# Queueing the side work of ScalarE and VectorE behind the weight chunk where it is traced, in a decoder-trunk kernel at S = 256

## The chip, the core and the metric

The kernel runs on one core of a Trainium2 chip. Its time is the device time of one execution in microseconds (us); where several runs are given, the median is used. Profiles come from a single profiled execution of the kernel.

## What is computed

One decoder layer on a 256 x 2048 float32 input (weights float32 too), then a final RMSNorm:

```python
u = rms_norm(x, attn_norm)
proj = u @ w_in                  # split: fox q|k|v|f, MLA latents, GDN q|k|v, z, b, a, three gates
o_fox = fox_mixer(...)           # 8 heads, causal softmax with cumulative forget-gate bias
o_mla = mla_mixer(...)           # 8 heads, latents projected up, rotary part, causal softmax
o_gdn = gdn_mixer(...)           # short conv, SiLU, gated delta rule in chunks of 64, norm * silu(z)
gates = sigmoid(gate)            # three gates of D_MODEL columns
merged = gates[0]*(o_fox @ w_branch[0]) + gates[1]*(o_mla @ w_branch[1]) + gates[2]*(o_gdn @ w_branch[2])
x = x + merged @ w_out
h = rms_norm(x, mlp_norm)
x = x + square(relu(h @ w_up)) @ w_down      # d_ff = 8192
return rms_norm(x, final_norm)
```

## The kernel before

The work is a stream of weight chunks. A chunk is two row tiles of 128 by up to 512 columns of a weight matrix (512 KB). For each, `gemm` (its body runs from L228 to L258) issues one load `raw` on the SP queue (L240, four buffers), rounds it on ScalarE to `wh` (L243, three buffers) and takes the rest `wl = raw - wh` on VectorE (L244, three buffers). TensorE then runs 12 matmuls for it: two row tiles of the weight, two 128-row tiles of the activation, and the three products `uH*wh` (L249), `uH*wl` (L250) and `uL*wh` (L251), which give back the float32 product. There are 590 chunks, numbered c0 to c589 here: the latents and the small columns of w_in (c0 to c23), the fox columns (c24 to c85, with the MLA projections between them), the z columns (c86 to c109, 344 to 360 columns wide), the GDN columns (c110 to c157), the gate columns (c158 to c253), the three branches by four column blocks (c254 to c301), w_out (c302 to c333), and four times w_up and w_down (from c334).

All other work is side work. It is written as generators, and `weave` takes one step of a generator after each chunk of the main stream:

```python
def weave(main, side):
    for _ in main:
        next(side, None)
```

Two more paths lead into the stream. The evacuation of a finished block (`evac`) is traced in `gemm` right after its last chunk. And `later(steps, f)` puts a callback off by so many chunks; `tick` calls it. The order in which a program is written (traced) is not the order in which an engine runs it: a scheduler with a model of the engines' times places each instruction of an engine's list, so a step may stand some chunks earlier on its engine than where it was traced. Each engine then runs its own list strictly in order, so an instruction that waits for a transfer holds up all that stand behind it on that engine, weight casts included.

The places that matter below:

- `turned` (L1043 to L1049) turns a 256 x 512 block so that its columns lie on partitions: VectorE transposes 32 x 32 blocks, POOL's queue writes them to DRAM (`turn`, L1045) and reads them back in four pieces (`zy`, L1048), and `later(TURN, ...)` with TURN = 9 hands the result on, to `halves_of` (L1057 on ScalarE casts the high half, for `mH`, `hH` and `dH`) or, behind w_out, to `gained` (L1100 on ScalarE multiplies by the norm's gain) and then `halves_of`.
- The delta-rule generator `gdn`: `E` holds decays that come back from DRAM by a broadcast load and are used by VectorE at L762. A loop of L838 and L840 on VectorE solves 16 rows step by step; its result goes to DRAM (`td`, L844) and back in eight pieces (`DT`, L854), both on POOL's queue, and VectorE takes it at L863 (`D`), on which 32 x 32 matmuls at L871 wait.
- The gates: `gate_evac` (L986) scales a block by `rstd` (ScalarE L319 for 12 of the 24 evacuations, VectorE L321 for the other 12) and stores it to `gd` (L987, POOL's queue). In the branch stage `evac` loads a gate back (L1066), applies the sigmoid (L1067, ScalarE) and multiplies.
- Fox attention runs as a side generator: bias at L655 (VectorE), scores at L385 and L391 (VectorE), exponent at L388 (ScalarE), transposes at L399 (evacuated by ScalarE) and output at L406 (ScalarE).
- `reload` brings the fox and the MLA output back from DRAM (`of`, `om`, 1 MB each, L1017), and L1084 loads x again for the residual (`xx`, two of 1 MB, POOL's queue).

Of the kernel before, what the change touches and what calls it, by code (L numbers as in the profile page):

```python
# [3 lines left out]

# [53 lines left out]
def decoder_kernel(ctx: ExitStack, tc: tile.TileContext, x, attn_norm, w_in, fox_fgate_bias, mla_q_norm,  # L58
# [30 lines left out]
    def t2(s="t2", dt=F32):  # L89
        return tp.tile([P, 512], dt, tag="t2", name=nm(s), bufs=8)  # L90
# [118 lines left out]
    CK = 2  # L209

    pending = []

    def later(steps, f):

# [2 lines left out]
    def tick():  # L217
        for p in pending:
            p[0] -= 1
        while pending and pending[0][0] <= 0:  # L220
            pending.pop(0)[1]()

    def by_tile(f):

        return lambda k, t: f(k)[:, t * P:(t + 1) * P]

    def gemm(lhsH, lhsL, W, row0, KT, blocks, evac, pair=False):

        ks = {}
        order = [(bi, kc) for bi in range(len(blocks)) for kc in range(0, KT, CK)]  # L230
        if pair:
            order.sort(key=lambda o: (max(o[0], 1), o[0] < 2 and o[1] >= LATE))
        for bi, kc in order:
            c0, n = blocks[bi]
            if kc == 0:
                ks[bi] = [pm.tile([P, 512], F32, tag="mm", name=nm("mm")) for _ in range(2)]
            ps = ks[bi]
            raw = wp.tile([P, CK, 512], F32, tag="raw", name=nm("raw"), bufs=4)
            r0 = row0 + kc * P
            nc.sync.dma_start(out=raw[:, :, :n], in_=W[r0:r0 + CK * P, c0:c0 + n].rearrange("(k p) n -> p k n", p=P))  # L240
            wh = wp.tile([P, CK, 512], F32R, tag="wh", name=nm("wh"), bufs=3)
            wl = wp.tile([P, CK, 512], F32R, tag="wl", name=nm("wl"), bufs=3)
            A.copy(out=wh[:, :, :n], in_=raw[:, :, :n])  # L243
            V.tensor_tensor(out=wl[:, :, :n], in0=raw[:, :, :n], in1=wh[:, :, :n].bitcast(F32), op=ALU.subtract)  # L244
            for kk in range(CK):
                k = kc + kk
                for t in range(2):
                    last = k == KT - 1
                    PE.matmul(ps[t][:, :n], lhsT=lhsH(k, t), rhs=wh[:, kk, :n], start=(k == 0), stop=False)  # L249
                    PE.matmul(ps[t][:, :n], lhsT=lhsH(k, t), rhs=wl[:, kk, :n], start=False, stop=False)  # L250
                    PE.matmul(ps[t][:, :n], lhsT=lhsL(k, t), rhs=wh[:, kk, :n], start=False, stop=last)  # L251
            tick()
            if kc + CK == KT:
                for t in range(2):
                    evac(bi, t, ps[t][:, :n])
            yield
# [28 lines left out]
            for _ in g:  # L285
                pass

    def weave(main, side):

        for _ in main:  # L290
            next(side, None)

    def wait(n):
        return range(n)
# [7 lines left out]
    def w_cols(blocks, evac):  # L302
        return gemm(by_tile(uH), by_tile(uL), w_in, 0, 16, blocks, evac)
# [12 lines left out]
    def scaled_evac(o, i, t):  # L316
        evc[0] += 1
        if evc[0] % 2:
            A.activation(out=o, in_=i, func=AF.Copy, scale=rstd[:, t:t + 1])  # L319
        else:  # L320
            V.tensor_scalar(out=o, in0=i, scalar1=rstd[:, t:t + 1], scalar2=None, op0=ALU.mult)  # L321
# [394 lines left out]
    def gdn():  # L716
# [38 lines left out]
        yield  # L755
        nc.gpsimd.dma_start(out=E, in_=gcd.unsqueeze(0).broadcast_to([P, 16 * P]))
        Ev = E.rearrange("p (u i) -> p u i", u=16)
        for _ in wait(5):
            yield
        for g in range(0, 16, 4):  # L760
            for u in range(g, g + 4):
# [89 lines left out]
        for b in range(4):  # L851
            for f in range(2):
                r0 = 32 * b + 16 * f
                nc.gpsimd.dma_start(out=DT[r0:r0 + 16, :, 32 * b:32 * b + 32], in_=tdv[f, b])  # L854
        for _ in wait(9):
            yield


# [124 lines left out]
    def gates(b0, b1):  # L983
        def gate_evac(bi, t, ps):
            e = me("ge")
            scaled_evac(e, ps, t)  # L986
            nc.gpsimd.dma_start(out=gd[t * P:(t + 1) * P, (b0 + bi) * 512:(b0 + bi + 1) * 512], in_=e)  # L987

        return w_cols([(C_GATE + i * 512, 512) for i in range(b0, b1)], gate_evac)
# [3 lines left out]
    fox_cols = [(i * 512, 512) for i in range(6)]  # L993
    side = chain(x_prep(), load_vectors())
    next(side)
    weave(gemm_first(w_in, blocks[0][0], blocks[0][1], lat_evac), side)
    weave(w_cols(blocks[2:], lambda bi, t, ps: lat_evac(2, t, ps)), side)
    side = chain(mla_prep(), fox_decay())
    weave(w_cols(fox_cols[0:1], fox_evac_at(0)), side)
    run(mla_proj())  # L1000
# [11 lines left out]
    def reload(d, s, r):  # L1012
        H = big(s + "H", F32R).rearrange("p (h t) -> p h t", t=S)
        L = big(s + "L", F32R).rearrange("p (h t) -> p h t", t=S)
        o = big(s)
        r.extend((H, L))
        nc.sync.dma_start(out=o, in_=d)  # L1017
        o = o.rearrange("p (h t) -> p h t", t=S)
        for _ in wait(2):
            yield  # L1020
        for h in range(0, 8, 2):
            hs = slice(h, h + 2)
            A.copy(out=H[:, hs, :], in_=o[:, hs, :])
            V.tensor_tensor(out=L[:, hs, :], in0=o[:, hs, :], in1=H[:, hs, :].bitcast(F32), op=ALU.subtract)
            if h % 4:
                yield
# [34 lines left out]
    for n in range(4):  # L1061
        acc = [t2("acc") for _ in range(2)]
        for i, b in enumerate((2, 0, 1)):
            def evac(bi, t, ps, b=b, n=n, acc=acc, i=i):
                g = t2("gate")
                nc.gpsimd.dma_start(out=g, in_=gd[t * P:(t + 1) * P, b * DM + n * 512:b * DM + (n + 1) * 512])  # L1066
                A.activation(out=g, in_=g, func=AF.Sigmoid)  # L1067
                if i == 0:
                    V.tensor_tensor(out=acc[t], in0=ps, in1=g, op=ALU.mult)
                else:  # L1070
                    V.tensor_tensor(out=g, in0=ps, in1=g, op=ALU.mult)
                    V.tensor_tensor(out=acc[t], in0=acc[t], in1=g, op=ALU.add)
                if i == 2 and t == 1:
                    turned(acc, lambda y: halves_of(y, n, mHt, mLt))

            if n == 0 and b < 2:
                run(again[b])
            weave(gemm(by_tile(lambda k, b=b: o_b[b][0][:, k, :]), by_tile(lambda k, b=b: o_b[b][1][:, k, :]), w_branch[0, b], 0, 8,
                       [(n * 512, 512)], evac), chain(*again))


    x2 = [big(f"xx{t}") for t in range(2)]
    for t in range(2):
        nc.gpsimd.dma_start(out=x2[t], in_=x[t * P:(t + 1) * P, :])  # L1084
    hH, hL, hHt, hLt = hl_pair("h")
    ss2 = small([P, 2, 4], "ss2")

# [12 lines left out]
            A.activation(out=yv[:, k], in_=yv[:, k], func=AF.Copy, scale=gcol[:, 16 + 4 * n + k:17 + 4 * n + k])  # L1100
        halves_of(y, n, hHt, hLt)

    run(gemm(by_tile(mH), by_tile(mL), w_out[0], 0, 16, [(n * 512, 512) for n in range(4)], out_evac, True))
    r2 = rstd_of(ss2, 4, DM, "r2")
    r2s = small([P, 2], "r2s")
    V.tensor_tensor(out=r2s, in0=r2, in1=r2, op=ALU.mult)


    fg = big("fg")
    ss3 = small([P, 2, 4], "ss3")  # L1110
    for c in range(4):
        dH, dL, dHt, dLt = hl_pair("d")
        if c == 2:
            nc.sync.dma_start(out=fg, in_=final_norm.unsqueeze(0).broadcast_to([P, DM]))
        rr = {}

        def up_evac(n, t, ps):
# [3 lines left out]
            if t == 1:  # L1121
                turned([rr[0], rr[1]], lambda y: halves_of(y, n, dHt, dLt))

        run(gemm(by_tile(hH), by_tile(hL), w_up[0], 0, 16, [(c * 2048 + n * 512, 512) for n in range(4)], up_evac, c == 0))

        def down_evac(n, t, ps):
            xb = x2[t][:, n * 512:(n + 1) * 512]
# [69 lines left out]
```

## Time and profile before

| | us |
|---|---|
| median of 3 runs | 1701.19 |
| lowest, highest of them | 1699.45, 1702.70 |
| the profiled execution's own time | 1702.46 |
| its span from first to last instruction | 1700.7 |

| engine | busy, us | share of the span |
|---|---|---|
| PE (TensorE) | 1674.5 | 98% |
| VectorE (DVE) | 1037.1 | 61% |
| ScalarE (ACT) | 803.0 | 47% |
| POOL | 114.2 | 7% |

The mean granted clock of TensorE is 0.995 of full speed. The DMA engines moved 356.53 MB, 210 GB/s on the mean. Matmuls overlap in the records (each is shown with 0.39 us and the next starts some 0.23 us later), so the end of a matmul says less than the start of the next.

### The profile page before, as it was taken

How to read it: one execution, taken by the hardware profiler on the slowest of the kernel's cores; microseconds unless marked ns; L12 is line 12 of the kernel's file. 1: busy time of each engine (PE TensorE's matmuls, PEld its weight loads, DVE VectorE, ACT ScalarE, POOL GpSimd, SP SyncE). 2: the span in 40 equal slices, each digit the busy share in tenths (PEclk: the TensorE clock that was granted, in tenths of full speed). 3: DMA queues.
4: the chain of work that ended last, by engine and by line, in shares of the span. 5: the costliest groups of instructions: out<-in, count | busy, mean ns of one | idle time of the engine just before them, and what ended most of it. 6: DMA issues, size and time to landing. Idle time of an engine off the chain costs nothing.

```text
span 1700.7 us, 21432 instructions
## 1 busy us (share of the span) xinstructions
PE 1674.5 (98%) x7987; PEld 1403.7 (83%) x7987; DVE 1037.1 (61%) x1430; ACT 803.0 (47%) x1035; POOL 114.2 (7%) x204
## 2 busy tenths in 40 slices
PE   9999999999999999999999989999999999999997
PEld 9998889978788788888888778888888888888886
DVE  5755465677679845746666556555655556555655
ACT  5545446556534434544454545433443344434443
POOL 0000000000010100001110101100110011001100
PEclk9999999999999999999999999999999999999999
DMA  7765554766667755877887778756886688667763
GB/s 234 205 172 176 163 171 135 229 193 181 172 177 215 208 162 159 261 217 256 279 294 240 237 200 247 241 192 197 233 262 205 193 234 246 198 191 229 238 208 137
DMA packets 188601, 356.53 MB, mean 210 GB/s; under 512 B 17704, under 2 KB 38608, under 8 KB 187344
## 3 DMA queue, kind: packets, MB, share of 16 engines
q1 hardware_dynamic: 174592, 309.23, 59.9%
q0 software_dynamic: 13584, 45.39, 8.9%
q8 instruction: 62, 1.02, 0.3%
q10 hardware_dynamic: 320, 0.53, 0.1%
q14 instruction: 43, 0.35, 0.1%
HBM read 331.50 MB, written 23.61 MB: 209 GB/s over the span
## 4 chain that ended last, share of the span: by engine, by line
PE 83%; DMA 6%; issue 4%; DVE 4%; ACT 1%; POOL 1%; SPq 0%; DVEq 0%; ACTq 0%; POOLq 0%
PE mm L250 24%; PE mm L251 24%; PE mm L249 24%; DMA zy<-turn 3%; DVE wl L244 2%; ACT wh L243 1%; DVE fs L838 1%; POOL zy L1048 1%; DMA turn<-zy 1%; DMA raw<-in_w_down_dram 1%; DMA of<-of_d 1%; DMA E<-gcd 0%; PE bf L490 0%; PE bf L489 0%; PE bf L488 0%
## 5 line engine op out<-in xcount | busy, mean ns | idle before, releaser
L244 DVE TENSOR_TENSOR wl<-raw,wh 128x1024 fp32r<-128x1024 f32 (+3 forms) x552 | 662.6, 1204 | 501.6 <-ACT wh L243 498.2
L243 ACT CAST wh<-raw 128x1024 fp32r<-128x1024 f32 (+3 forms) x552 | 570.0, 1036 | 671.4 <-PE mm L251 624.6
L250 PE MATMUL mm<-wl,uH 128*128 128x512 f32 (+3 forms) x896 | 346.3, 387 | 2.1 <-DVE wl L244 2.0
L251 PE MATMUL mm<-wh,uL 128*128 128x512 f32 (+3 forms) x896 | 342.8, 383 | 0.0
L249 PE MATMUL mm<-wh,uH 128*128 128x512 f32 (+3 forms) x896 | 318.9, 386 | 1.2 <-ACT wh L243 1.2
L250 PE MATMUL mm<-wl,hH 128*128 128x512 f32 x512 | 200.4, 391 | 2.0 <-DVE wl L244 2.0
L251 PE MATMUL mm<-wh,hL 128*128 128x512 f32 x512 | 199.9, 390 | 0.0
L250 PEld LDWEIGHTS mm<-wl,uH 128*128 128x128 f32 x896 | 168.9, 188 | 32.9 <-DVE wl L244 3.5
L249 PEld LDWEIGHTS mm<-wh,uH 128*128 128x128 f32 x896 | 167.9, 188 | 31.4 <-ACT wh L243 1.7
L251 PEld LDWEIGHTS mm<-wh,uL 128*128 128x128 f32 x896 | 168.8, 188 | 29.6
L250 PE MATMUL mm<-wl,dH 128*128 128x512 f32 x480 | 187.0, 390 | 0.1
L251 PE MATMUL mm<-wh,dL 128*128 128x512 f32 x480 | 186.8, 389 | 0.0
L249 PE MATMUL mm<-wh,hH 128*128 128x512 f32 x512 | 179.2, 391 | 3.5 <-ACT wh L243 3.5
L249 PE MATMUL mm<-wh,dH 128*128 128x512 f32 x480 | 167.2, 389 | 0.0
L249 PEld LDWEIGHTS mm<-wh,hH 128*128 128x128 f32 x512 | 96.3, 189 | 24.4 <-ACT wh L243 4.6
L250 PEld LDWEIGHTS mm<-wl,hH 128*128 128x128 f32 x512 | 96.4, 188 | 23.8 <-DVE wl L244 3.7
L251 PEld LDWEIGHTS mm<-wh,hL 128*128 128x128 f32 x512 | 96.5, 189 | 20.0
L250 PEld LDWEIGHTS mm<-wl,dH 128*128 128x128 f32 x480 | 90.1, 188 | 19.6 <-DVE wl L244 0.9
L251 PEld LDWEIGHTS mm<-wh,dL 128*128 128x128 f32 x480 | 90.1, 188 | 18.7
L249 PEld LDWEIGHTS mm<-wh,dH 128*128 128x128 f32 x480 | 90.1, 188 | 18.6
L1048 POOL DMA_DIRECT2D zy<-turn x96 | 52.4, 553 | 100.1 <-ACT wh L243 37.7
L1045 POOL DMA_DIRECT2D turn<-zy x24 | 13.3, 556 | 657.6 <-DVE zy L1043 657.6
(420 smaller groups left out, 1762.3 us busy)
## 6 DMA issues: line engine op xcount, KB each, us to landing
raw<-in_w_in_dram SPq DMA_DIRECT2D x192, 512.0 KB, 3.9
raw<-in_w_up_dram SPq DMA_DIRECT2D x128, 512.0 KB, 4.4
raw<-in_w_down_dram SPq DMA_DIRECT2D x128, 512.0 KB, 4.5
raw<-in_w_branch_dram SPq DMA_DIRECT2D x48, 512.0 KB, 4.6
raw<-in_w_out_dram SPq DMA_DIRECT2D x32, 512.0 KB, 5.1
turn<-zy POOLq DMA_DIRECT2D x24, 512.0 KB, 3.3
zy<-turn POOLq DMA_DIRECT2D x96, 128.0 KB, 5.8
gd<-ge POOLq DMA_DIRECT2D x24, 256.0 KB, 4.6
```

The source lines that it names most:

```text
L243: A.copy(out=wh[:, :, :n], in_=raw[:, :, :n])
L244: V.tensor_tensor(out=wl[:, :, :n], in0=raw[:, :, :n], in1=wh[:, :, :n].bitcast(F32), op=ALU.subtract)
L249: PE.matmul(ps[t][:, :n], lhsT=lhsH(k, t), rhs=wh[:, kk, :n], start=(k == 0), stop=False)
L250: PE.matmul(ps[t][:, :n], lhsT=lhsH(k, t), rhs=wl[:, kk, :n], start=False, stop=False)
L251: PE.matmul(ps[t][:, :n], lhsT=lhsL(k, t), rhs=wh[:, kk, :n], start=False, stop=last)
L838: V.tensor_tensor(out=tmp[:, :, 0:i + 1], in0=T[:, :, 0:i + 1], in1=Nb[:, 0:i + 1, i].unsqueeze(1).broadcast_to([P, 16, i + 1]), op=ALU.mult)
L1045: nc.gpsimd.dma_start(out=d, in_=z)
L1048: nc.gpsimd.dma_start(out=y[32 * j:32 * j + 32].rearrange("a (g x) -> a g x", g=4), in_=dv[j])
```

## The change

`gemm` remembers the cast and the subtraction of the latest chunk. All side work that is traced afterwards, by `weave` and by `later`, is put behind them: an ordering edge makes the instructions of such a step follow `wh` on ScalarE's list and `wl` on VectorE's. It is a lower bound: the scheduler may still place them further back. The first two weaves (`x_prep`, `load_vectors`) are left free, and evacuations aren't bound. Besides, all 24 gate evacuations become one ScalarE sigmoid with `rstd` as its scale, and the sigmoids of the branch stage go; gate tiles are loaded before their block begins instead of in its evacuation; `of`, `om`, `xx` and the final gain come in pieces of 256 KB, one a step, `xx` on the SP queue instead of POOL's; and two counts of idle steps ahead of `E` and `D` change (5 to 7, 9 to 7).

```diff
+    anchor = []
+    @contextmanager
+    def behind():
+        with ExitStack() as st:
+            for i in anchor:
+                st.enter_context(tc.issue_after(i))
+            yield
...
         while pending and pending[0][0] <= 0:
-            pending.pop(0)[1]()
+            with behind():
+                pending.pop(0)[1]()
...
-            A.copy(out=wh[:, :, :n], in_=raw[:, :, :n])
-            V.tensor_tensor(out=wl[:, :, :n], in0=raw[:, :, :n], in1=wh[:, :, :n].bitcast(F32), op=ALU.subtract)
+            h = A.copy(out=wh[:, :, :n], in_=raw[:, :, :n])
+            l = V.tensor_tensor(out=wl[:, :, :n], in0=raw[:, :, :n], in1=wh[:, :, :n].bitcast(F32), op=ALU.subtract)
+            anchor[:] = [h.ins, l.ins]
...
-    def weave(main, side):
+    def weave(main, side, free=False):
         for _ in main:
-            next(side, None)
+            if free:
+                next(side, None)
+            else:
+                with behind():
+                    next(side, None)
...
-        for _ in wait(5):
+        for _ in wait(7):
...
-        for _ in wait(9):
+        for _ in wait(7):
...
             e = me("ge")
-            scaled_evac(e, ps, t)
+            A.activation(out=e, in_=ps, func=AF.Sigmoid, scale=rstd[:, t:t + 1])
...
-        nc.sync.dma_start(out=o, in_=d)
+        for q in range(0, 2048, 512):
+            nc.sync.dma_start(out=o[:, q:q + 512], in_=d[:, q:q + 512])
+            yield
...
-            def evac(bi, t, ps, b=b, n=n, acc=acc, i=i):
-                g = t2("gate")
-                nc.gpsimd.dma_start(out=g, in_=gd[t * P:(t + 1) * P, b * DM + n * 512:b * DM + (n + 1) * 512])
-                A.activation(out=g, in_=g, func=AF.Sigmoid)
+            gt = [t2("gate") for _ in range(2)]
+            for t in range(2):
+                nc.gpsimd.dma_start(out=gt[t], in_=gd[t * P:(t + 1) * P, b * DM + n * 512:b * DM + (n + 1) * 512])
+
+            def evac(bi, t, ps, n=n, acc=acc, i=i, gt=gt):
+                g = gt[t]
...
-    for t in range(2):
-        nc.gpsimd.dma_start(out=x2[t], in_=x[t * P:(t + 1) * P, :])
+    def load_x2():
+        for n in range(4):
+            for t in range(2):
+                nc.sync.dma_start(out=x2[t][:, n * 512:(n + 1) * 512], in_=x[t * P:(t + 1) * P, n * 512:(n + 1) * 512])
+                yield
```

How the lists move, at three places. First ScalarE behind w_out, around c333 to c342: `zy` at L1100 (L1124 after the change) is the gain on the turned block, `wh` the weight cast. Before:

```order
L243 CAST wh_8356<-raw_8354 128x1024
L243 CAST wh_8374<-raw_8372 128x1024
L243 CAST wh_8392<-raw_8390 128x1024
L1100 ACTIVATE zy_8245<-zy_8245,gcol 128x8x32 x4
L243 CAST wh_8455<-raw_8453 128x1024
...
L243 CAST wh_8553<-raw_8551 128x1024
L243 CAST wh_8573<-raw_8571 128x1024
L1100 ACTIVATE zy_8414<-zy_8414,gcol 128x8x32 x4
L243 CAST wh_8591<-raw_8589 128x1024
L1057 CAST hH_7755<-zy_8414 128x4x128 x2
L243 CAST wh_8609<-raw_8607 128x1024
```

And after:

```order
L253 CAST wh_8362<-raw_8360 128x1024
L253 CAST wh_8380<-raw_8378 128x1024
L253 CAST wh_8443<-raw_8441 128x1024
L1124 ACTIVATE zy_8233<-zy_8233,gcol 128x8x32 x4
L253 CAST wh_8469<-raw_8467 128x1024
...
L253 CAST wh_8579<-raw_8577 128x1024
L253 CAST wh_8597<-raw_8595 128x1024
L1124 ACTIVATE zy_8402<-zy_8402,gcol 128x8x32 x4
L253 CAST wh_8623<-raw_8621 128x1024
L1074 CAST hH_7735<-zy_8402 128x4x128 x2
L253 CAST wh_8641<-raw_8639 128x1024
```

The third block's gain (zy_8245, now zy_8233) stands one weight cast further back, behind that of c334 instead of c333; the fourth's (zy_8414, now zy_8402) two, behind c342 instead of c340. Of the same four, the first moves from c322 to c324 and the second stays behind c326. Likewise `mH` moves from c273, c285, c297, c311 to c274, c286, c298, c311, and the last `dH` of each group by one or two chunks. The VectorE transposes that start a turn stay at their chunks.

Second VectorE and POOL around the solve of the delta rule (L863, after the change L878, takes `DT`). Before, on VectorE:

```order
L838 TENSOR_TENSOR fs_4589<-NT_4510 128x512
L840 TENSOR_REDUCE NT_4510<-fs_4589 128x16
L244 TENSOR_TENSOR wl_5319<-raw_5316,wh_5318 128x1024
L321 TENSOR_SCALAR ge_5293<-mm_5137,rstd_115 128x512
L244 TENSOR_TENSOR wl_5337<-raw_5334,wh_5336 128x1024
L244 TENSOR_TENSOR wl_5361<-raw_5358,wh_5360 128x1024
L863 STREAM_TRANSPOSE D_5352<-DT_5134 32x16x32
L244 TENSOR_TENSOR wl_5379<-raw_5376,wh_5378 128x1024
```

And after:

```order
L853 TENSOR_TENSOR fs_4589<-NT_4510 128x512
L254 TENSOR_TENSOR wl_5257<-raw_5254,wh_5256 128x1024
L855 TENSOR_REDUCE NT_4510<-fs_4589 128x16
L254 TENSOR_TENSOR wl_5275<-raw_5272,wh_5274 128x1024
L254 TENSOR_TENSOR wl_5301<-raw_5298,wh_5300 128x1024
L254 TENSOR_TENSOR wl_5325<-raw_5322,wh_5324 128x1024
L878 STREAM_TRANSPOSE D_5316<-DT_5134 32x16x32 x2
L254 TENSOR_TENSOR wl_5343<-raw_5340,wh_5342 128x1024
```

The loop ends two chunks earlier (before the subtraction of c198, now behind that of c196), and the first use of `DT` comes two chunks earlier as well (behind c201, now c199); the number of subtractions between them stays at three, but the gate evacuation is gone. On POOL's queue `td` had two gate stores (L987) behind it and then the eight `DT`; now `DT` follows `td` directly. `E` at L762 (L777) stays behind the subtraction of c124.

Third ScalarE in the gate columns, after the change (c174 to c183; L710 is the SiLU of the short convolution, L1001 the gate's sigmoid, `ACT_TABLE_LOAD` what stands ahead of a function whose table isn't loaded):

```order
L710 ACT_TABLE_LOAD
L710 ACTIVATE y_4408<-y_4408 128x512
L253 CAST wh_4822<-raw_4820 128x1024
L1001 ACT_TABLE_LOAD
L1001 ACTIVATE ge_4790<-mm_4620,rstd_115 128x512
L253 CAST wh_4842<-raw_4840 128x1024
L341 COPY vtok_129<-vb_4422 128x2x256
L699 ACTIVATE y_4429<-cv_4428,cw 128x256
L1001 ACTIVATE ge_4793<-mm_4621,rstd_115 128x512
```

Before, L319 stood at the place of the first L1001, with no table load there, and there was none at the second. Over the whole list of ScalarE the table loads go from 7 to 13. Fox attention's side work, spread before from c76 to c101, stands from c87 to c101 after the change.

## Rows read from the trace of the kernel before

**Rows 1.** The page: busy time of each engine over the span.

```profile
PE 1674.5 (98%) x7987; PEld 1403.7 (83%) x7987; DVE 1037.1 (61%) x1430; ACT 803.0 (47%) x1035; POOL 114.2 (7%) x204
```

**Rows 2.** Waits of PE over the whole span: engine, operation, line, what it waited for; us in total, times, longest.

```profile
PE mm L250 <- DVE wl L244: 6.1, 10, 1.2
PE mm L249 <- ACT wh L243: 5.5, 5, 1.9
...
PE pO L871 <- DMA DT<-td: 1.5, 1, 1.5
```

**Rows 3.** Waits of ACT over the whole span, same columns.

```profile
ACT wh L243 <- PE mm L251: 624.6, 391, 5.2
```

**Rows 4.** Timelines of ACT in the branches, w_out and the first w_up (start, length, engine, line, operation, and in brackets the idle time before it and what ended it).

```profile
841.49 1.05 ACT L243 CAST wh<-raw 128x1024 fp32r<-128x1024 f32 x1 [1.67 <-PE mm L251]
847.40 1.14 ACT L1057 CAST mH<-zy 128x512 fp32r<-128x512 f32 x2 [4.85 <-DMA zy<-turn]
...
879.58 1.15 ACT L1057 CAST mH<-zy 128x512 fp32r<-128x512 f32 x2 [2.84 <-DMA zy<-turn]
...
960.37 1.71 ACT L1100 ACTIVATE zy<-zy,gcol 128x256 f32<-128x256 f32 x4 [4.72 <-DMA zy<-turn]
...
983.86 1.71 ACT L1100 ACTIVATE zy<-zy,gcol 128x256 f32<-128x256 f32 x4 [6.12 <-DMA zy<-turn]
...
1005.54 1.71 ACT L1100 ACTIVATE zy<-zy,gcol 128x256 f32<-128x256 f32 x4 [5.91 <-DMA zy<-turn]
```

**Rows 5.** Timelines of PE at the same places and in the later w_up, the rows with a wait.

```profile
850.06 0.73 PE L249 MATMUL mm<-wh,omH 128*128 128x512 f32 x2 [0.45 <-ACT wh L243]
851.32 0.50 PE L250 MATMUL mm<-wl,omH 128*128 128x512 f32 x1 [0.53 <-DVE wl L244]
...
986.55 0.73 PE L249 MATMUL mm<-wh,hH 128*128 128x512 f32 x2 [1.93 <-ACT wh L243]
987.82 0.50 PE L250 MATMUL mm<-wl,hH 128*128 128x512 f32 x1 [0.53 <-DVE wl L244]
...
1008.23 0.73 PE L249 MATMUL mm<-wh,hH 128*128 128x512 f32 x2 [1.53 <-ACT wh L243]
1009.49 0.50 PE L250 MATMUL mm<-wl,hH 128*128 128x512 f32 x1 [0.53 <-DVE wl L244]
...
1403.91 0.50 PE L250 MATMUL mm<-wl,hH 128*128 128x512 f32 x1 [0.38 <-DVE wl L244]
...
1578.93 0.50 PE L250 MATMUL mm<-wl,hH 128*128 128x512 f32 x1 [0.53 <-DVE wl L244]
```

**Rows 6.** Windows of 4 us in the first w_up: busy us (and instructions) of each engine, granted clock of TensorE as a share of full speed, DMA share, GB/s.

```profile
1010.00:1014.00 4.00, 4.00 (x12) 3.09 (x12) 2.91 (x4) 1.44 (x3) 0.00 (x0) 0.57 0.70 176
1014.00:1018.00 4.00, 4.00 (x19) 3.31 (x18) 1.70 (x2) 1.78 (x2) 0.00 (x0) 1.00 0.79 259
```

**Rows 7.** Timelines of DVE, POOL and PE where `DT` is awaited, in that order.

```profile
580.72 0.69 DVE L840 TENSOR_REDUCE NT<-fs 128x16 f32<-128x512 f32 x1
...
583.12 2.57 DVE L244 TENSOR_TENSOR wl<-raw,wh 128x1024 fp32r<-128x1024 f32 x2
592.52 0.70 DVE L863 STREAM_TRANSPOSE D<-DT 32x512 f32<-32x512 f32 x1 [6.83 <-DMA DT<-td]
...
581.95 0.54 POOL L844 DMA_DIRECT2D td<-NT  x1 [20.34 <-DVE NT L840]
...
583.50 0.54 POOL L987 DMA_DIRECT2D gd<-ge  x1 [0.48 <-DVE ge L321]
584.98 4.48 POOL L854 DMA_DIRECT2D DT<-td  x8 [0.94 <-issue]
...
593.47 0.47 PE L871 MATMUL pO<-D,E 32*32 32x32 f32 x10 [1.52 <-DMA DT<-td]
594.38 0.50 PE L250 MATMUL mm<-wl,uH 128*128 128x512 f32 x1 [0.43 <-DVE wl L244]
```

**Rows 8.** Timelines of DVE where `E` is awaited.

```profile
357.74 2.44 DVE L762 TENSOR_SCALAR E<-E,gc 128x128 f32<-128x128 f32 x12 [3.52 <-DMA E<-gcd]
```

**Rows 9.** Groups by line over the whole span (busy us, mean ns of one | idle before, releasers): the sigmoids of the branch stage and the gate evacuations on VectorE.

```profile
L1067 ACT ACTIVATE gate<-gate 128x512 f32<-128x512 f32 x24 | 14.0, 623 | 1.5 <-DMA gate<-gd 1.5
L321 DVE TENSOR_SCALAR ge<-mm,rstd 128x512 f32<-128x512 f32 x12 | 9.0, 746 | 6.4 <-PE mm L251 3.8 <-DMA gd<-ge 2.6
```

**Rows 10.** Timeline of ACT around a table load of the z columns.

```profile
300.68 0.77 ACT L243 CAST wh<-raw 128x688 fp32r<-128x688 f32 x1 [1.13 <-PE mm L251]
301.46 1.28 ACT L709 ACT_TABLE_LOAD   x1
302.76 0.99 ACT L709 ACTIVATE zg<-mm,rstd 128x348 f32<-128x348 f32 x2
```

**Rows 11.** Groups of ACT from 255 to 325 us (fox attention's end, the z columns), same columns as rows 9.

```profile
L243 ACT CAST wh<-raw 128x696 fp32r<-128x696 f32 (+2 forms) x29 | 23.7, 819 | 21.3 <-PE mm L251 16.3 <-issue 3.2 <-ACT pp L388 1.0
L388 ACT ACTIVATE pp<-sl,st 128x256 f32<-128x256 f32 (+1 forms) x9 | 4.2, 462 | 2.6 <-DVE st L385 2.6
L399 ACT COPY pT<-pT 128x384 f32<-128x384 f32 x7 | 3.3, 467 | 0.8 <-PE pT L397 0.8
L406 ACT COPY of<-po 128x256 f32<-128x256 f32 x8 | 3.0, 372 | 1.0 <-PE po L405 1.0
```

**Rows 12.** DMA issues (KB each, median us from issue to landing): x for the residual.

```profile
xx<-in_x_dram POOLq DMA_DIRECT2D x2, 1024.0 KB, 10.5
```

More of the change, by code (lines that the diff above doesn't have):

```diff
@@ L1 @@
 import math
-from contextlib import ExitStack
+from contextlib import ExitStack, contextmanager
 from itertools import chain
@@ L995, in decoder_kernel @@
     next(side)
-    weave(gemm_first(w_in, blocks[0][0], blocks[0][1], lat_evac), side)
-    weave(w_cols(blocks[2:], lambda bi, t, ps: lat_evac(2, t, ps)), side)
+    weave(gemm_first(w_in, blocks[0][0], blocks[0][1], lat_evac), side, True)
+    weave(w_cols(blocks[2:], lambda bi, t, ps: lat_evac(2, t, ps)), side, True)
     side = chain(mla_prep(), fox_decay())
@@ L1101, in gained @@
         halves_of(y, n, hHt, hLt)
-    run(gemm(by_tile(mH), by_tile(mL), w_out[0], 0, 16, [(n * 512, 512) for n in range(4)], out_evac, True))
+    weave(gemm(by_tile(mH), by_tile(mL), w_out[0], 0, 16, [(n * 512, 512) for n in range(4)], out_evac, True), load_x2())
     r2 = rstd_of(ss2, 4, DM, "r2")
@@ L1109, in decoder_kernel, with load_fg @@
     fg = big("fg")
+    def load_fg():
+        for q in range(0, DM, 512):
+            nc.sync.dma_start(out=fg[:, q:q + 512], in_=final_norm[q:q + 512].unsqueeze(0).broadcast_to([P, 512]))
+            yield
     ss3 = small([P, 2, 4], "ss3")
@@ L1112, in decoder_kernel @@
         dH, dL, dHt, dLt = hl_pair("d")
-        if c == 2:
-            nc.sync.dma_start(out=fg, in_=final_norm.unsqueeze(0).broadcast_to([P, DM]))
         rr = {}
@@ L1122, in up_evac @@
                 turned([rr[0], rr[1]], lambda y: halves_of(y, n, dHt, dLt))
-        run(gemm(by_tile(hH), by_tile(hL), w_up[0], 0, 16, [(c * 2048 + n * 512, 512) for n in range(4)], up_evac, c == 0))
+        weave(gemm(by_tile(hH), by_tile(hL), w_up[0], 0, 16, [(c * 2048 + n * 512, 512) for n in range(4)], up_evac, c == 0),
+              load_fg() if c == 2 else iter(()))
         def down_evac(n, t, ps):
```

## The prediction, made before the changed kernel had run

> **What bounds the kernel now.** Read the page's first part first: PE is busy in 1674.5 of 1700.7 us [rows 1]. So nothing that another engine does faster can help unless PE stands still for it, and the whole prize is small. Next come PE's own waits [rows 2]: it waited 6.1 us for subtractions (L244), 5.5 for casts (L243) and 1.5 for `DT`, 13.1 together, in stops of at most 1.9 us. ACT, on the other side, waits 624.6 us for PE [rows 3]: in the steady stream a cast takes 1.05 us and then ACT is idle for 1.67 (at 841.49) [rows 4], so a chunk lasts 2.72.
>
> A cast is thus not late by want of speed. It is late where an instruction ahead of it on ACT's list waits for a transfer. The timelines of ACT show this: at 847.40 `mH` has waited 4.85 us for a turned block, at 983.86 and 1005.54 the gain (L1100) 6.12 and 5.91 [rows 4]. Put beside them what PE lost [rows 5]: 0.45 + 0.53 = 0.98, 1.93 + 0.53 = 2.46 and 1.53 + 0.53 = 2.06. Each wait less its loss gives 3.87, 3.66 and 3.85. The wait of 2.84 at 879.58 has no loss beside it. So three buffers of `wh` forgive **some 3.7 us of waiting** on ACT, and what goes beyond is lost one for one. This figure prices most of the change.
>
> **Part by part, against the profiled execution's 1702.46 us.**
>
> *Turned blocks used later.* The start of each turn stays at its chunk; only its user moves back, by one chunk (2.72 us) or two. The third block's gain then waits 6.12 - 2.72 = 3.4, below 3.7: its loss of 2.46 goes. The fourth waits 5.91 - 5.44 = 0.5: its 2.06 go. `mH` of the second block waits 4.85 - 2.72 = 2.1: its 0.98 go. The last `dH` of a group moves back as well; PE lost 0.38 at 1403.91 and 0.53 at 1578.93 to it, 0.9 together [rows 5]. The second block's gain stays behind c326, so I give nothing for its wait of 4.72 [rows 4]. Sum: -6.4. What if a wait shrinks by less than a chunk, because the transfer lands later too? The third has only 0.3 us to spare, so I keep an end at which its 2.46 shrink to about 1.2.
>
> *The clock after the fourth.* Right behind 1009.49 the granted clock is 0.57 on the mean from 1010 to 1014, and PE runs 12 matmuls there against 19 in the next 4 us [rows 6]; that is a stretch at the lower of its two levels (1.2 GHz against 2.4). Seven matmuls less at 4.00 / 19 = 0.21 us are 1.5 us. The row shows the drop directly behind stops of 1.53 and 0.53 us; without them I expect none. **-1.5**, with 0 as the other end, since the same drop might come elsewhere.
>
> *`DT`.* VectorE waits 6.83 us for it and PE loses 1.52 + 0.43 = 1.95 [rows 7]. From the loop's end (580.72 + 0.69 = 581.41) to the end of the wait are 11.1 us. Without the two stores ahead of `DT` (2 x 0.54 of issue and 0.48 of waiting, 1.56) it would be 9.5. The place of `DT` on VectorE was at 583.12 + 2.57 = 585.69, and two chunks earlier is 580.25. If the loop ends right behind the subtraction of c196, two chunks before its old end and no sooner, 576 to 577, the wait is 5.3 to 6.3 and the loss 0.4 to 1.4 (6.83 - 1.95 = 4.9 are forgiven here). If VectorE is ahead by the evacuations it no longer has (9.0 us over the whole gate stage [rows 9], some 4 up to there, with another side step that moved behind), the loop ends at 574, the wait is 3.2 and the loss 0. I take 0.4, near the second since VectorE is the late engine in that loop: **-1.5**, between -0.5 and -1.95.
>
> *`E`.* It waits 3.52 us behind the same subtraction [rows 8] and its place doesn't change. 0, though the diff adds two idle steps there.
>
> *Gates.* The branch stage loses 24 sigmoids, 14.0 us of ACT [rows 9], and VectorE 12 evacuations, 9.0 us. Both engines wait for PE there, so this is worth 0. The gate columns gain 12 evacuations on ACT and, with the SiLU between them, most of the six extra table loads. A load is 1.28 us, begins where the cast before it ends (300.68 + 0.77) and the activation begins at 302.76, 0.02 behind its end [rows 10]. Load and sigmoid are 1.28 + 0.62 = 1.9, 0.2 over ACT's idle 1.67 in a chunk. Over the tightest three chunks, with convolution and copy beside them, I count ACT behind by 1 to 2 us: under 3.7, so 0. Each load exposed whole would be 6 x 1.28 = 7.7; that is a rival.
>
> The Trainium skill, in "ScalarE: Activation LUTs", section "What ACT_TABLE_LOAD costs", sets 2.66 us for every switch, a drain of 1.38 beside the load's 1.28; by it (an estimate from that page) the six switches would be 16 us of ACT. This trace agrees with the load and shows no drain: the rows on either side leave 0.02 us.
>
> *Fox attention pressed together.* Its side work ran over 26 chunks, now over 15 (c87 to c101), in the narrow z columns. A head costs ACT two exponents, a copy of the transposes and one of the output: 2 x 0.46 + 0.47 + 0.37 = 1.76 us [rows 11]. In the densest five chunks (c93 to c97) the list holds about five heads and two table loads: 9 + 2.6, with the casts (0.77 each, 3.9) and the accumulator reads about 17 to 18 us, against some 16 that PE needs. So ACT falls 2 to 4 us behind, and the margin is 3.7 at wide chunks and smaller at narrow ones. Cost **+0.5**, from 0 to 3. It isn't 0 for certain as ACT's idle of 21.3 us in this stretch [rows 11] lies mostly in chunks that are not the dense ones.
>
> *x on the SP queue, reload in pieces.* x moves from ahead of w_out into its first eight chunks: 2 MB more beside the weights. The two took 10.5 us each to land from POOL's queue [rows 12] with no loss on PE near them. In pieces ahead of weight loads they delay a load by some of their own 256 KB each; loads run up to four chunks ahead. **+0.2**, up to 1.5. The pieces of `of` and `om` on the same queue: **+0.3**, up to 1. The final gain in pieces: 0, it lies under w_up.
>
> **Sum.** -6.4 - 1.5 - 1.5 + 0.5 + 0.2 + 0.3 = -8.4, 1694.06 for an execution like the profiled one. That one is 1.27 above the median of the runs shown (1701.19), so as a median **1692.8**. Worst ends together (turn -5.1, clock 0, `DT` -0.5, costs +5.5) leave the time as it was; best ends (`DT` -1.95, costs 0) give 1691.3, and 1689.8 with the 1.5 to 1.7 by which the runs shown lie to either side of their median. The ends will hardly all fall to one side, so the forecast's own range is 1689.8 to 1697.5.
>
> **Rivals.**
>
> 1. *The stops keep their place.* The edges are lower bounds: `E` and the second gain stand where they stood. If the third gain and `DT` lose their slack (a later landing takes what the later place gave), only the fourth (2.06 + 1.5) and the small ones (0.98 + 0.9) are won, less 1.0 of costs: -4.4 to -2, so 1697 to 1699. For it: the third has 0.3 us to spare. Against: the turns start at unchanged chunks, and POOL's queue has less on it. Chance 0.14; a third of it still counts as faster.
>
> 2. *Table loads on the path.* The loads alternate with SiLU just where the convolution also uses ACT. Exposed whole, 7.7: 1700.5. For it: load and sigmoid don't fit the 1.67 us of a chunk. Against: the 3.7 us of margin, and the stretch recovers in the next chunk. The same section's neighbour in the Trainium skill ("ScalarE: Activation LUTs", "Table sets: the hidden batching unit") says to batch activations by set, and speaks against this change; by its 2.66 us each the estimate would be 1708.8. Chance 0.06.
>
> 3. *Slower: fox attention on the path.* Each head is a chain from PE over VectorE, ACT and back to PE. With the heads pressed into narrow chunks, ACT may be later than its margin in every one of them; then PE waits for each head's ACT work, 8 x 1.76 = 14 us, and the time is 1692.8 + 14 - 0.5 = 1706. It decides itself where a cast in c90 to c100 is over 3.7 us late; five heads in five chunks come near that. Half of it would be 1699. For it: the count above. Against: the order of PE moves along with the others, so PE has its own fox matmuls and casts ahead. Chance 0.08, slower in most of it.
>
> **How the numbers follow.** The forecast has 0.72, the rivals 0.14, 0.06 and 0.08. About 0.2% (3.4 us) is what a measurement of this kernel can tell from no change: faster is below 1697.8, slower above 1704.6. Faster: 0.72 + 0.04 = 0.76, less 0.02 for the forecast's worst ends, 0.74; slower: 0.06 and 0.01 of table loads, 0.07; same: 0.19. The range goes from 1689.8, the best ends, to 1700.0, which takes in rival 1 and half of rivals 2 and 3, and leaves out under 2 in 10.
>
> **What would show it.** In the profile after: ACT's longest waits for `zy` under 4.8 us, with 4.7 left at the second block alone; no half clock near 1010 us; PE's waits for L253 and L254's casts and subtractions down from 11.6 to about 5, most of it at `E` and at the second block; `DT` awaited under 5 us. ACT's busy time should hardly change (loads +7.7, twelve more evacuations at 0.62 +7.4, sigmoids -14.0), with 13 table loads and no stop of PE beside them. The forecast is wrong if PE stops between 255 and 300 us (fox), if stops appear at 470 to 530 us (table loads), or if the third gain still waits over 5 us.

## The result, and the profile after

The changed kernel takes **1693.24 us** (median of 6 runs, 1691.08 to 1696.24); the kernel before, run beside it, 1702.71 (6 runs, 1699.45 to 1704.96). The ratio is 0.9948, 95% interval 0.9934 to 0.9961. Forecast were 1692.8 us, so the time was right, in part by luck: between the two profiles (the table below) 7.9 us of costs that the forecast didn't have, 4.2 of them at one place, stand against 5.1 us of gains that it didn't have either. Four executions in the series further down took 2088 to 4358 us; they count in the medians but not in the ratios, and a ratio is not the quotient of the medians beside it.

The profiled execution of the changed kernel took 1696.24 us, the slowest of the six, with a span of 1694.5; so the two profiles lie 6.2 apart, the medians 9.5. The page's first part, against [rows 1], and PE's longest waits, against [rows 2]:

```profile
PE 1672.8 (99%) x7987; PEld 1403.8 (83%) x7987; DVE 1027.7 (61%) x1418; ACT 807.7 (48%) x1029; POOL 113.2 (7%) x202
```

```profile
PE mm L261 <- DVE wl L254: 3.7, 7, 1.1
PE mm L260 <- ACT wh L253: 2.8, 2, 2.6
PE fc L640 <- issue: 2.8, 1, 2.8
...
PE pO L886 <- DVE D L878: 0.7, 1, 0.7
```

The waits for casts and subtractions fell from 11.6 to 6.5 us. A new one stands among them: `fc`, 2.8 us, put down to "issue" (nothing that the profile shows). To see where the time went, set the start of the n-th weight matmul in both traces side by side (7176 in each; number 4200, counted from 0, starts at 1013.5 before and at 1010.2 after) and follow the difference, which ends at -5.6. It is sorted by chunk here, with the forecast's terms for the same stretch. A half-clock stretch is one at the lower of TensorE's two levels (1.2 GHz against 2.4).

| stretch | change of the difference, us | what lies there | forecast |
|---|---|---|---|
| c0 to c5 | -1.9 | a half-clock stretch at 10 us that only the profile of before has | 0 |
| c5 to c35 | +4.2 | the stop at `fc`, a half-clock stretch behind it | none |
| c35 to c125 | 0.0 | fox attention pressed together | +0.5 |
| c125 to c140 | +1.1 | `E` | 0 |
| c140 to c190 | 0.0 | table loads | 0 |
| c190 to c245 | +1.4 | `DT`, one more half-clock stretch, reload | -1.2 |
| c245 to c300 | -1.5 | `mH` | -1.0 |
| c300 to c350 | -6.5 | the gains, x, no half clock behind them | -5.8 |
| c350 to the end | -2.4 | `dH` | -0.9 |

This is one profile of each kernel. A second profile of the changed kernel, under the experiments, agrees with it at `fc` and at the gain step of the third and fourth block, and has other sizes at `E`, `DT` and the second block's.

The timelines of ACT show the waits for turned blocks now, against [rows 4]: 4.85 has become 1.02, 4.72 has become 3.37, 6.12 has become 4.52, and the fourth gain doesn't wait at all.

```profile
851.05 1.14 ACT L1074 CAST mH<-zy 128x512 fp32r<-128x512 f32 x2 [1.02 <-DMA zy<-turn]
...
962.32 1.71 ACT L1124 ACTIVATE zy<-zy,gcol 128x256 f32<-128x256 f32 x4 [3.37 <-DMA zy<-turn]
...
986.75 1.71 ACT L1124 ACTIVATE zy<-zy,gcol 128x256 f32<-128x256 f32 x4 [4.52 <-DMA zy<-turn]
...
1007.51 1.71 ACT L1124 ACTIVATE zy<-zy,gcol 128x256 f32<-128x256 f32 x4
```

And PE's timelines, against [rows 5, 7]; behind 995 us no stop is left that the rows record:

```profile
365.52 0.74 PE L260 MATMUL mm<-wh,uH 128*128 128x512 f32 x2 [2.65 <-ACT wh L253]
366.62 0.50 PE L261 MATMUL mm<-wl,uH 128*128 128x512 f32 x1 [0.36 <-DVE wl L254]
...
590.88 0.34 PE L886 MATMUL pO<-D,E 32*32 32x32 f32 x6 [0.69 <-DVE D L878]
592.66 0.50 PE L261 MATMUL mm<-wl,uH 128*128 128x512 f32 x1 [0.41 <-DVE wl L254]
...
970.40 0.50 PE L261 MATMUL mm<-wl,mH 128*128 128x512 f32 x1 [1.12 <-DVE wl L254]
...
989.45 0.73 PE L260 MATMUL mm<-wh,hH 128*128 128x512 f32 x2 [0.15 <-ACT wh L253]
990.71 0.50 PE L261 MATMUL mm<-wl,hH 128*128 128x512 f32 x1 [0.53 <-DVE wl L254]
994.23 0.50 PE L261 MATMUL mm<-wl,hH 128*128 128x512 f32 x1 [0.46 <-DVE wl L254]
```

The new stop: PE's timeline at `fc` (the cumulative sum of the forget gates), and VectorE's row that writes its operand `nl`.

```profile
83.27 1.03 PE L145 MATMUL tr<-cst,cqn 128*128 128x128 f32 x8
87.07 0.36 PE L640 MATMUL fc<-nl,cst 128*128 128x16 f32 x2 [2.77 <-issue]
```

```profile
86.79 0.17 DVE L637 SCALAR_TENSOR_TENSOR nl<-fz,sfp 128x16 f32<-128x16 f32 x1
```

Before, the same VectorE instruction ran at 58.53 us, 27 us ahead of `fc`:

```profile
58.53 0.17 DVE L622 SCALAR_TENSOR_TENSOR nl<-fz,sfp 128x16 f32<-128x16 f32 x1
```

So "issue" has an owner: `fc` starts 0.11 us behind the end of `nl`. The step `fox_decay` is chained into the weave of the first fox column. Bound to the chunks, its chain of small VectorE instructions moved from c17 to c23 to c29 to c34, and PE's list has `fc` where it was.

Windows of 4 us around the stops (columns as in [rows 6]):

```profile
84.00:88.00 4.00, 1.23 (x12) 1.02 (x11) 3.72 (x12) 2.16 (x5) 0.00 (x0) 1.00 0.66 193
88.00:92.00 4.00, 4.00 (x24) 4.00 (x23) 0.00 (x0) 1.19 (x2) 0.00 (x0) 0.57 0.26 75
593.00:597.00 4.00, 4.00 (x19) 2.72 (x18) 2.70 (x3) 0.17 (x1) 0.00 (x0) 0.57 0.77 178
...
1010.00:1014.00 4.00, 4.00 (x19) 3.33 (x18) 3.57 (x4) 3.00 (x5) 0.00 (x0) 1.00 0.77 220
```

At 1010 the clock stays whole and 19 matmuls run where 12 ran [rows 6], 7 x 0.23 = 1.6 us. Other half-clock stretches have come in this profile, behind the stop at `fc` and behind that at `DT`.

### The profile page after: what moved, and what is told of

It reads as the page before. It is cut to its first block, busy times and chain, and to the rows that moved or that the text cites. A ratio compares the mean times of both kernels' runs of the same rounds, so it can differ in the third digit from the quotient of the medians.

```text
span 1694.5 us, 21459 instructions
## 1 busy us (share of the span) xinstructions
PE 1672.8 (99%) x7987; PEld 1403.8 (83%) x7987; DVE 1027.7 (61%) x1418; ACT 807.7 (48%) x1029; POOL 113.2 (7%) x202
## 3 DMA queue, kind: packets, MB, share of 16 engines
q8 instruction: 62, 1.02, 0.2%
## 4 chain that ended last, share of the span: by engine, by line
PE 93%; DMA 3%; DVE 2%; issue 1%; ACT 1%; POOL 0%; SPq 0%; DVEq 0%; POOLq 0%; ACTq 0%
PE mm L261 28%; PE mm L262 27%; PE mm L260 27%; DVE wl L254 1%; DMA raw<-in_w_in_dram 1%; DMA E<-gcd 1%; DMA raw<-in_w_up_dram 1%; PE bf L503 0%; PE bf L504 0%; PE bf L505 0%; PE mm L1188 0%; PE mm L1187 0%; PE mm L1186 0%; PE po L419 0%; PE pg L828 0%
```

## The experiments

Theory A: the edges on `later` bring the gain, because they set behind which chunk an instruction that waits for a turned block stands; the edges on the weaves earn nothing and cost the stop at `fc`. Against it stood others, named with each run.

**The later edges alone** (kernel before, with)

```diff
-            pending.pop(0)[1]()
+            with behind():
+                pending.pop(0)[1]()
```

> The kernel before with one edit: the callbacks of later() are put behind the latest chunk's cast and subtraction; weaves, gates, loads and idle counts as before. Theory A (the later edges bring the gain, the bound weaves cost time): 9 to 11 us under the kernel before (its stops at 849, 984, 1006, 1403 and 1578 us gone, no half clock near 1010), thus at or below the full change. Theory B (the bound weaves and the gate edit bring half of it): only 4 to 6 us under the kernel before.

1694.65 us against 1702.58, ratio 0.9948 (0.9930 to 0.9967): 8 to 9 us, a little less than A wanted and over B's 4 to 6 (the interval's weak end is 5.6 us, B's best 6). This one edit gives as much as the whole change. There is no half clock but at the end and no stop from 1000 us on. The third gain still waits, as it does in the change, and PE lost 0.50 + 0.50 there; `DT` cost 1.92 + 0.43, much as before.

```profile
982.61 1.71 ACT L1111 ACTIVATE zy<-zy,gcol 128x256 f32<-128x256 f32 x4 [4.06 <-DMA zy<-turn]
...
1003.23 1.70 ACT L1111 ACTIVATE zy<-zy,gcol 128x256 f32<-128x256 f32 x4
```

But near 849 us a stop stays, for another reason than before; ACT and VectorE there:

```profile
847.64 0.63 ACT L1078 ACTIVATE gate<-gate 128x512 f32<-128x512 f32 x1 [5.66 <-DMA gate<-gd]
```

```profile
848.31 0.69 DVE L1080 TENSOR_TENSOR acc<-mm,gate 128x512 f32<-128x512 f32 x1 [5.06 <-ACT gate L1078]
```

The second gate tile's load stands behind the four `zy` on POOL's queue, which wait for `turn`. ACT's sigmoid now waits for it where `mH` had waited for `zy`. In its profile PE lost 2.2 us at such places between 815 and 890 us.

**The weave edges alone** (kernel before, the first two weaves left free as in the change, with)

```diff
-            next(side, None)
+            with behind():
+                next(side, None)
```

> The kernel before with one edit: side steps of weave() are put behind the chunk (first two weaves free, as in the change); later() and all else as before. Theory A: 0 to 5 us above the kernel before: a stop of TensorE of 2 to 3 us near 84 us at the forget gate's cumulative sum, which was none before, and all stops at 849 to 1009 us as before; DT one chunk earlier gives at most 1 us. Theory B: 3 to 5 us under the kernel before.

1705.5 against 1702.58, ratio 1.0023 (1.0005 to 1.0041): slower, as A says. The stop at `fc` is there:

```profile
87.37 0.37 PE L639 MATMUL fc<-nl,cst 128*128 128x16 f32 x2 [2.77 <-issue]
```

`DT`, which was to gain up to 1 us, cost 1.67 + 1.32 instead of 1.52 + 0.43, and stops of 0.53 + 0.53 near 1283 us and 1.08 + 0.53 near 1631 us are new in this profile. So `fc` need not be all that these edges cost here.

**Everything but the edges**

```diff
-            for i in anchor:
+            for i in ():
```

> The whole change with its ordering edges taken out (behind() adds none): gates as ScalarE sigmoids, gate tiles loaded ahead, loads in pieces and on the SP queue, idle counts 7 and 7. Theory A: 0 to 3 us under the kernel before: stops at 849 and from 962 to 1009 us as before, DT's stop down to under 1 us, no stop at 84 us. Theory B (the gate and load edits take the load off the turned blocks' way): 4 us or more under it.

1700.8 against 1702.58, ratio 0.9988 (0.9974 to 1.0001): at most a little faster, A. `DT`'s stop was 1.19 + 0.31 us, over the 1 us expected. The third gain stands behind c333 as before, and the stop behind it is whole, 3.03 us:

```profile
983.10 1.70 ACT L1124 ACTIVATE zy<-zy,gcol 128x256 f32<-128x256 f32 x4 [7.41 <-DMA zy<-turn]
```

Against A's expectation the fourth's is down to 0.41 us, and there is no stop at 849 us, only one of 0.52 at 815; the ninth experiment comes back to that.

**The first fox column's weave left free** (the whole change, with)

```diff
-    weave(w_cols(fox_cols[0:1], fox_evac_at(0)), side)
+    weave(w_cols(fox_cols[0:1], fox_evac_at(0)), side, True)
```

> The whole change, with the one weave of the first fox column (which holds the forget gate's decay) left free, so that the decay's VectorE steps stand from c17 to c23 again instead of c29 to c34. Theory A: the stop of 2.77 us near 84 us goes, and the half clock near 88 us with it: 2.5 to 4.5 us under the full change. Theory B (the stop is made up for later, or is chance in the one profile): within 1 us of the full change.

1690.64 against 1702.58, ratio 0.9924 (0.9905 to 0.9942). The change itself gave 0.9948 and 0.9937 in its two series, so this is 2 to 4 us under it, though the intervals overlap. The row bears out the cause: no wait at `fc`, and full clock from 84 to 92 us.

```profile
84.20 0.29 PE L640 MATMUL fc<-nl,cst 128*128 128x16 f32 x2
```

**Four buffers of `wh`** (kernel before, with this at the three places that make a `wh`)

```diff
-            wh = wp.tile([P, CK, 512], F32R, tag="wh", name=nm("wh"), bufs=3)
+            wh = wp.tile([P, CK, 512], F32R, tag="wh", name=nm("wh"), bufs=4)
```

> The kernel before with one edit: four buffers of wh instead of three. The casts then run one chunk (2.72 us) further ahead, and the list of ScalarE has the second and third gain behind the same chunks as before (c326, c333), the first and fourth gain, mH and the last dH one chunk later. Theory A (what counts is the chunk behind which the list puts the waiting instruction): the stop of 2.5 us near 984 us stays whole although ScalarE has a buffer more, those at 849, 1006, 1403 and 1578 us go: 4 to 6 us under the kernel before, with the longest wait for zy near 8.8 us instead of 6.1. Theory C (three buffers forgive 3.7 us, four forgive 6.4, wherever the instruction stands): the stop near 984 us goes too and that near 962 us: 8 us or more under it.

1703.15 against 1704.91, ratio 0.9992 (0.9977 to 1.0007): no clear gain. The test was the third gain, behind c333 in both lists. ACT waits longer for it, and so does PE (2.46 before):

```profile
988.14 1.70 ACT L1100 ACTIVATE zy<-zy,gcol 128x256 f32<-128x256 f32 x4 [6.83 <-DMA zy<-turn]
```

```profile
990.83 0.80 PE L249 MATMUL mm<-wh,hH 128*128 128x512 f32 x1 [3.40 <-ACT wh L243]
992.08 0.80 PE L250 MATMUL mm<-wl,hH 128*128 128x512 f32 x1 [0.46 <-DVE wl L244]
```

The stops near 1006, 1403 and 1578 us, whose instructions the list had moved by a chunk, went. The third gain speaks against C: it stayed behind its chunk, and its stop stayed. But the second gain, behind c326 in both lists, speaks for C. It waited 7.03 us instead of 4.72, and PE lost only 0.77 instead of 1.95, so 6.3 us were forgiven there. Ahead of the third gain, ACT had waited 4.38 us for a weight load, so it was not ahead there by the buffer that it had more:

```profile
964.16 1.71 ACT L1100 ACTIVATE zy<-zy,gcol 128x256 f32<-128x256 f32 x4 [7.03 <-DMA zy<-turn]
...
980.25 1.05 ACT L243 CAST wh<-raw 128x1024 fp32r<-128x1024 f32 x1 [4.38 <-DMA raw<-in_w_out_dram]
```

```profile
968.13 0.50 PE L250 MATMUL mm<-wl,mH 128*128 128x512 f32 x1 [0.77 <-DVE wl L244]
```

So this run doesn't decide between A and C; it shows that a fourth buffer alone brings no clear gain. The sizes expected were missed, the wait (8.8) and the gain (4 to 6 us). The stop near 849 us, which was to go, had 0.69 + 0.76 us, and there were new ones at 287 us (2.03, `pT`), at 594 to 598 us (1.48 and 2.35, `D`) and at 896 us (1.02).

**All weaves free, later edges kept** (the whole change, with)

```diff
-            if free:
+            if True:
```

> The whole change with all weaves left free and the later edges kept. Theory A (the edges of the weaves earn nothing, they cost the stop near 84 us): within 1.5 us of the change with the first fox column free, 10 to 13 us under the kernel before. Theory B (binding the side steps earns part of the gain at E, DT or in the fox heads): 3 us or more slower than that version.

1688.89 against 1704.91, ratio 0.9918 (0.9897 to 0.9939), beside 0.9924 for the version with the first fox column free: the same. By the ratio that is 14 us under the kernel before, more than the 10 to 13 expected. The edges of the weaves earn nothing that these runs can tell. From the version without any edge (third experiment, 0.9988) this one differs in the edges on `later` alone: some 12 us, more than the 8 to 9 that the same edges gave on the kernel before.

**Users moved back further** (first fox column free, and these; the first `wait` stands ahead of `E`, the second ahead of `D`)

```diff
-TURN = 9
+TURN = 11
...
-        for _ in wait(7):
+        for _ in wait(13):
...
-        for _ in wait(7):
+        for _ in wait(10):
```

> The change with the first fox column free, and three counts raised: the callbacks of turned blocks after 11 chunks instead of 9 (second gain behind c328 instead of c326, third c336), E used after 13 steps instead of 7 (behind c126 instead of c124), D after 10 instead of 7 (behind c201 instead of c199). Theory A: the stops at 358 to 365 (2.2 us), 585 to 588 (1.4), 960 to 966 (2.1) and 985 to 989 us (0.9) shrink to under 1 us together: 4 to 7 us under the version with the first fox column free, 15 to 19 under the kernel before. Theory D (a user moved back makes its own followers late: the row loop behind E, the matmuls behind D, hH for the last row tiles of w_up): stops of the same size appear behind them and the time stays within 2 us of that version.

**1683.0 against 1704.91**, ratio 0.9880 (0.9856 to 0.9904): faster than both kernels and, at some 20 us by the ratio, at or over A's size; not D. PE's waits over the whole span:

```profile
PE mm L283 <- ACT uH L149: 1.4, 1, 1.4
PE warm L123 <- DVE ones L108: 1.1, 1, 1.1
PE mm L260 <- ACT wh L253: 0.9, 1, 0.9
PE mm L261 <- DVE wl L254: 0.5, 1, 0.5
```

No stop is left at `E`, `DT` and the gains. What remains near 695 us (0.93 + 0.53) stands behind the reload of `of`:

```profile
693.25 0.62 ACT L1040 CAST ofH<-of 128x512 fp32r<-128x512 f32 x1 [4.13 <-DMA of<-of_d]
```

**The change again, and two parts undone on the same chip.**

> The whole change again, beside the next two on one chip. Theory A (the stop near 84 us and the places of the others belong to the program): stops of TensorE at the same chunks as in its first profile, 2.7 to 2.8 us at the forget gate's sum among them; 8 to 11 us under the kernel before. Theory E (the stop near 84 us was chance): none there.

1694.21 against 1703.22, ratio 0.9937 (0.9922 to 0.9953). `fc` stops PE for 2.76 us again, so that stop isn't chance, but this time no half clock lies behind it. The others stand at the same chunks in other sizes: 2.2 us at `E` instead of 3.7, 1.66 + 0.42 + 0.26 around `DT` instead of 0.69 + 0.41 + 0.15, and at the second gain 0.40 + 0.53 + 1.11 instead of 1.12.

```profile
590.16 0.34 PE L886 MATMUL pO<-D,E 32*32 32x32 f32 x6 [1.66 <-DVE D L878]
```

```profile
961.75 1.71 ACT L1124 ACTIVATE zy<-zy,gcol 128x256 f32<-128x256 f32 x4 [4.76 <-DMA zy<-turn]
```

The third gain waited 4.12 us with 0.53 + 0.50 behind it, and the fourth didn't wait: there the two profiles agree.

Gate tiles loaded in the evacuation:

```diff
-            for t in range(2):
-                nc.gpsimd.dma_start(out=gt[t], in_=gd[...])
...
                 g = gt[t]
+                nc.gpsimd.dma_start(out=g, in_=gd[...])
```

> The whole change, but each gate tile loaded in its block's evacuation as before, not ahead of the block (the stored sigmoids stay). On POOL's queue the second tile's load then stands behind the four zy pieces again, which wait for turn. Theory A (the later edges alone only move the stop near 849 us: the products with the gate wait in its place): stops of 0.5 us or more return near 815, 850 and 885 us, 1.5 to 3 us in sum, and the time is that much over the full change. Theory F (the early load is worth nothing, as forecast): no stops there, within 0.5 us of TensorE's idle time of the full change.

1695.64, ratio 0.9959 (0.9942 to 0.9976), 1.4 us over the change with overlapping intervals. A's sizes were wrong here. VectorE waits up to 4.42 us for the gate,

```profile
850.95 0.69 DVE L1087 TENSOR_TENSOR acc<-mm,gate 128x512 f32<-128x512 f32 x1 [4.42 <-DMA gate<-gd]
```

but PE loses 0.04 and 0.14 us there; F was right about the stops. VectorE's wait is within what the buffers forgive. So in the branch stage it is most likely the stored sigmoid, with nothing left on ACT between gate and product, that takes the stops of the first experiment away (2.2 us there). No run has the stored sigmoids alone; without the edges (third experiment) 0.52 us was left in this stage. The early load by itself is worth no more than these runs can tell.

x on POOL's queue, issued ahead of w_out:

```diff
-                nc.sync.dma_start(out=x2[t][:, n * 512:(n + 1) * 512], in_=x[...])
+        nc.gpsimd.dma_start(out=x2[t], in_=x[t * P:(t + 1) * P, :])
```

> The whole change, but x for the residual loaded as before, two transfers of 1 MB on POOL's queue ahead of w_out. Theory A (x in pieces costs nothing): ScalarE's waits of 3 to 4.5 us for weights of w_out near 911 to 920 us go, TensorE has no stop more or less there, within 1 us of the full change. Theory G (2 MB ahead of w_out's weights cost time that the stops don't show, or slow the last turned block): 1.5 us or more under the full change.

1695.88, ratio 0.9942 (0.9924 to 0.9961): the same as the change. ACT's waits for w_out's weights, up to 4.5 us in the change, are gone, and PE's stops are as they were. The 2 MB on SP cost nothing that shows.

## Why the prediction was right, and where it failed

*Turned blocks and the clock: right in kind, undersized.* Forecast were -7.9 with the clock, and the last three stretches of the table give -10.4 (forecast for them -7.7, with x). The single stops didn't fall as priced. The third gain still waited 4.52 instead of 3.4, and PE lost 0.15 + 0.53 + 0.46 there, so the worse end (2.46 shrinking to about 1.2) came about, in both profiles. The second, given 0 because it stays behind c326, waited 1.35 less in the first profile and PE's 1.95 shrank to 1.12; in the second profile it waited 4.76 and PE lost 2.04, so the 0 stands. The sum came out bigger for another reason, the way stops were counted. A matmul is recorded with 0.39 us and the next one normally starts 0.23 later, so the idle time in brackets leaves out 0.16 us at every stop. Recorded stops from 849 us on fell from 8.5 to 2.3, and eight stops fewer are another 1.3; with 1.6 of clock that is 9.1 of the 10.4. What the rest is isn't shown. The clock's other end, that the drop comes elsewhere, came about over the whole span: the profile of before and the first of the change both have three half-clock stretches ahead of the one at the end.

*The margin of 3.7 us is not a constant.* The forecast took it from three waits. The fourth wait that cost PE something was the second gain's, and it was left out. It forgave less, 4.72 - 1.95 = 2.8; PE's rows of it, before:

```profile
963.07 0.73 PE L249 MATMUL mm<-wh,mH 128*128 128x512 f32 x2 [0.35 <-ACT wh L243]
964.33 0.50 PE L250 MATMUL mm<-wl,mH 128*128 128x512 f32 x1 [0.53 <-DVE wl L244]
968.46 0.50 PE L250 MATMUL mm<-wl,mH 128*128 128x512 f32 x1 [1.07 <-DVE wl L244]
```

After the change the third gain forgave 4.52 - 1.14 = 3.4. The figure has to be read for each place.

*`mH`: right sum, wrong cause.* The forecast gave the 0.98 to the later place. The first experiment shows that the place alone turned the wait for `zy` into one for the gate. By the third and ninth it takes the stored sigmoids as well, which the forecast had priced at 0.

*The failed step: the list of what moves.* The forecast went through fox attention, gates, `E`, `DT` and the turned blocks, but left out `fox_decay`, whose move to c29 to c34 made `nl` 28 us later while PE's `fc` stayed. It was thus put at nothing without a reason. It cost 2.8 us and, in the first profile, a half-clock stretch behind it (24 matmuls from 88 to 92 us, where the version without the stop has 35). The fourth experiment got that back.

*`DT`: -1.5 forecast, no gain that two profiles agree on.* In the first the loop ended at 580.01 us, behind c196's subtraction, the slow end that the forecast had not taken. VectorE waited 5.54 us (the forecast's sign was under 5), and PE lost 0.69 + 0.41 at `DT` and 0.15 ahead of it, 0.7 less than before; a half-clock stretch at 593 us took that back. In the second profile VectorE waited 6.51 us, and PE lost 2.3, no less than the 1.95 before.

```profile
579.33 0.68 DVE L855 TENSOR_REDUCE NT<-fs 128x16 f32<-128x512 f32 x1
...
589.92 1.43 DVE L878 STREAM_TRANSPOSE D<-DT 32x512 f32<-32x512 f32 x2 [5.54 <-DMA DT<-td]
```

*`E`: 0 forecast, +1.1 in the first profile.* VectorE waited 4.79 us instead of 3.52 [rows 8]. Its load took 9.0 us to land against 7.9 before, and 7.9 again in the second profile. PE lost 2.8 us there before, 3.7 in this profile, 2.2 in the second, and 0.9 to 2.3 in those of the fourth, ninth and tenth experiment, which don't touch `E`: a spread from profile to profile, with no sign of the edit.

*Fox, table loads, x, reload: right.* No stop lies between c35 and c125 nor beside the loads of c167 to c183, though ACT has 13 loads; the 1.0 us set aside for fox, x and reload was too much. Six loads exposed whole would have been 7.7 us. By the Trainium skill ("ScalarE: Activation LUTs", "Table sets: the hidden batching unit") activations should be batched by set. Here alternating cost nothing that the trace shows; ACT was busy for 48% of the span and waited for PE in most chunks.

*The rivals.* Edges as mere lower bounds (rival 1) were real at `E` and the second gain, which kept their places. The slower rival had PE wait for side work that was moved back; that came true, though not in the fox heads and over ACT, but at `fc`, where PE waited for VectorE.

## What to carry to other kernels

Where PE is the bound and buffers are few, look for the instruction that waits for a transfer ahead of a cast. Its wait less the margin at that place is what PE loses. A later place on the list took such stops away here or halved them, where a fourth buffer brought no clear gain. When an edit binds or moves side work wholesale, list every step that it moves and, for each, who waits for its result, down to 16-column sums. Read the sizes of small stops from more than one profile. Keep such an edit to the places that need it: the edges on the callbacks alone gave as much as the whole change, the edges on the weaves gave a stop, and with the first fox column free and three counts raised the gain was 1.2%.

## What the runs showed of the hardware

The same program has half-clock stretches in different number and place from profile to profile. One of them, seen in a 4 us window as a granted clock of 0.57, cost about 1.6 us. They lie behind PE stops of about 1 to 3 us and behind the 32 x 32 matmuls of 600 to 614 us; the best version drops there (0.57 from 603 to 607 us) with no stop ahead of it. Some were longer: in the fifth experiment's profile the windows from 594 to 606 us have 0.60, 0.50 and 0.61. Some stops had none behind them (`fc` in the second profile), and what decides it stays open. Besides that one, the best version's profile has one at the very end. A table load stood between a cast and an activation with no more than its 1.28 us [rows 10].
